# A hybrid decoder step: sixteen prompt-only FFN tiles, the sample rows' chain pinned step by step between the prompt's matmuls, and the prompt's query blocks attended in the order 3, 2, 1, 0

## The chip, the cores and the metric

The kernel runs on one core of one Trainium2 chip. The metric is the device time in microseconds (us) of one execution, taken as the median of three runs. Beside these runs stands one profiled execution, from which every duration below is read. The engines are called PE (TensorE; PEld is its weight load), DVE (VectorE), ACT (ScalarE), POOL (GpSimd) and SP (SyncE, which only issues DMAs).

## The reference, cut to what matters

One layer of a decoder is computed for two groups of tokens with the same weights: a prompt of 512 tokens, and a sample group of 8 sequences with 4 new tokens each (32 rows), which have 4096 cached positions behind them in a paged cache.

```python
def hybrid_layer(x, pos0, attend, lru_buf, lru_h0, ffn_buf, lw):
    ...
    h = rmsnorm(x, norm_mix_g)
    q, k, v, qi, ki, wi, xl, gl, ga, gb = split_cols(h @ w_in, IN_SPLITS)
    ...
    y_a = attend(q, k, v, qi, ki, wi).reshape(B, T, ATTN_WIDTH) @ w_proj_a
    xc, lru_buf_new = causal_dwconv(xl, lru_buf, lru_conv_w, lru_conv_b)
    hl, h_last = rg_lru(xc, lru_h0, lru_wa, lru_ba, lru_wx, lru_bx, lru_lambda)
    y_b = (hl * jax.nn.gelu(gl)) @ w_proj_b
    x = x + (jax.nn.sigmoid(ga) * y_a + jax.nn.sigmoid(gb) * y_b) @ w_out
    h = rmsnorm(x, norm_ffn_g)
    ua, ub = split_cols(h @ w_up, (D_FF, D_FF))
    uc, ffn_buf_new = causal_dwconv(ua, ffn_buf, ffn_conv_w, ffn_conv_b)
    x = x + (jax.nn.gelu(uc) * ub) @ w_down
```

`attend` is sparse in both groups. A small indexer scores every position, and each query attends only to its best ones: of the 512 prompt positions the best 128, of the 4100 sample positions the best 256. For a sample row the 256 selected keys and values lie anywhere in `cache_k` and `cache_v`, so they have to be gathered row by row (512 numbers each, 8 heads of 64). D is 1024, the FFN is 3072 wide, and the outputs also hold keys, values and states.

## The kernel before, in words

Everything is one program for a tile framework, which schedules the instructions of each engine by a simulated timeline: `tc.high_priority(n)` raises the priority of what stands inside, and `tc.issue_after(x)` puts an instruction behind x. Each engine then takes its instructions in that fixed order; each tile pool has a number of buffers, and a load waits until its buffer is free.

Large matmuls are three passes over operands split into a high and a low part: a chunk of weights is loaded on SP's queue into `wr` (3 buffers), ACT casts it to `wh` (L167), DVE subtracts to get `wl` (L168; two buffers each), and PE multiplies high by high, high by low and low by high.

In the order of time:

1. *Projections, recurrence, index scores, prompt attention.* Prompt attention is done in units of a query block i (128 rows; block i sees i + 1 blocks of keys) and some heads: four heads in a unit for i = 0 and 1, two for i = 2 and 3. A unit multiplies queries and keys (L542), adds the mask (L933), makes probabilities (L935 to L942), transposes them (L948) and multiplies them with the values (L963). The units of i = 0, 1 and 2 run as a pipeline among other projections; then comes the projection of the recurrent branch with its gates, and the four units of i = 3 at a higher priority. Beside this, DVE selects each sample row's 256 positions.
2. *proj_a and w_out.* The attended rows are split into `yahi` and `yalo`, multiplied with w_proj_a in eight tiles (L1005 to L1007), gated, and multiplied with w_out (L233 to L235). Meanwhile the selected positions are turned into row numbers `idx`: PE spreads them by one-hot matmuls (L867), and DVE (L871) and ACT (L873) reduce 64 blocks of them.
3. *Norm and prompt-only FFN tiles.* Of the 24 tiles of 128 FFN columns the first NP = 12 are computed for the prompt's 512 rows alone: `form_p` (L258 to L260) makes 24 matmuls of 512 columns for each of the two halves of w_up, DVE convolves (L1243, L1245) and gates (L1259), and after each four tiles `form_a` multiplies with their rows of w_down (2 x 48 matmuls of 512 columns, L233 to L235) and DVE adds the result to the rows (L1265).
4. *The sample rows' chain*, beside stage 3 at a low priority (PRIO // 10): for each of the 32 sample rows (a "key" below is one such row with its 256 gathered cached keys) POOL issues two gathers of 128 cached rows (L1067), which wait until the norms' last power on POOL (`normed`) is past. The scores of a key are made in one of three ways, by a table of letters: P (10 keys), PE transposes the rows (L1100), ACT copies them (L1101), PE multiplies (L1109); A (6 keys), DVE multiplies with the broadcast query (L1118) and ACT sums over 64 elements (16 instructions, L1122); D (16 keys), DVE multiplies (L1118) and DVE reduces (L1125). Then follow a softmax for each half of the rows (L1131 to L1150), eight steps of values with eight gathers each (L1174), folds (L1162, L1185), w_proj_a and w_out for these rows and their norm. Only then are the sample rows ready for the FFN.
5. *Shared tiles.* The other 12 tiles are computed for prompt and sample rows together: `form_b` (L248 to L250) makes 24 matmuls of 256 columns and 24 of 288 for each half of w_up. What the sample rows still lack of the first 12 tiles is made by `rows_by_columns` (L278; bursts of 32 small matmuls over 512 KB of weights, loaded on SP's queue at L271 into `sw`, three buffers), one step of `sample_steps` behind each shared tile. At the end come the first half of w_down for the 12 tiles, its last half (L1421, L1428 to L1430) and the final norm.

Of the kernel before, what the change touches and what calls it, by code (L numbers as in the profile page):

```python
# [18 lines left out]
D = 1024  # L19
SEQ = 512  # L20
# [8 lines left out]
NP = 12  # L29
# [67 lines left out]
def build(tc, I, O, dbg=None, mark=lambda n: None):  # L97
# [16 lines left out]
    with outer:  # L114
# [32 lines left out]
        WAYS = "PDDPPDDPDDDPADAPDDDPDAAPDDAPDDDP"  # L147
# [67 lines left out]
        def form_a(w, nk, a_hi, a_lo, a_s, col0, ncol, kc):  # L215
# [5 lines left out]
            for k0 in range(0, nk, kc):  # L221
# [7 lines left out]
                for t in range(4):  # L229
                    sl = slice(t * 128, (t + 1) * 128)  # L230
                    for k in range(kc):
# [3 lines left out]
                        T.matmul(out[t], a_lo[:, kk, sl], hi[:, k, :], start=False, stop=kk == nk - 1)  # L235
# [17 lines left out]
        def form_p(w, col0, a_hi, a_lo, ps, first=None):  # L253

            b = ps()
            _, hi, lo = first or columns(w, 8, col0)
            for k in range(8):
                T.matmul(b, hi[:, k, :], a_hi[:, k, :SEQ], start=k == 0, stop=False)  # L258
                T.matmul(b, hi[:, k, :], a_lo[:, k, :SEQ], start=False, stop=False)  # L259
                T.matmul(b, lo[:, k, :], a_hi[:, k, :SEQ], start=False, stop=k == 7)  # L260
            return b

        def rows_by_columns(a_s, nk, mk, w, col0, burst):
# [3 lines left out]
            for k0 in range(0, nk, burst):  # L267
                rows = []
                for k in range(k0, k0 + burst, 2):
                    raw = mk((128, 2, 512))  # L270
                    nc.sync.dma_start(raw, w[k * 128:(k + 2) * 128, col0:col0 + 512].rearrange("(k p) c -> p k c", p=128))  # L271
                    rows += [raw[:, 0], raw[:, 1]]
                order = list(range(k0, k0 + burst))[::-1]
                head = None
                for k in order:
                    for c in range(4):
                        with tc.issue_after(head.ins) if head else ExitStack():
                            m = T.matmul(b[32 * c:32 * c + 32, :128], a_s[:, k, :], rows[k - k0][:, c * 128:(c + 1) * 128],  # L278
                                         start=k0 == 0 and k == order[0], stop=k0 + burst == nk and k == order[-1],
                                         tile_position=(0, 32 * c))  # L280
                        head = head or m
# [121 lines left out]
        kih = mp.tile([128, SEQ], F32R, name="kih")  # L403
# [434 lines left out]
        with tc.high_priority(PRIO // 10):  # L838
# [15 lines left out]
            scr2 = CW((128, 512), F16)  # L854
            for h4 in range(2):
# [5 lines left out]
                for t in range(4):  # L861
# [3 lines left out]
                    for j in range(2):  # L865
                        for bi in range(4):
                            T.matmul(bs[j][:, bi * 128:(bi + 1) * 128], oh[32 * t:32 * t + 32, bi, j * 128:(j + 1) * 128],  # L867
                                     M[32 * t:32 * t + 32, h4 * 4 + bi, 0:128], start=True, stop=True, tile_position=(32 * t, 0))
# [9 lines left out]
                    V.scalar_tensor_tensor(ix, phys, float(PG), slot, op0=ALU.mult, op1=ALU.add)  # L878

            vms = CW((128, 2, 288), BF16)  # L880
# [589 lines left out]
```

## Time and profile before

| | us |
|---|---|
| three runs | 1070.83, 1074.62, 1075.09 |
| median | 1074.62 |
| profiled execution | 1077.11 |
| its span (first to last instruction) | 1075.0 |
| PE busy in the span | 1007.3 |
| DVE busy | 695.9 |
| ACT busy | 425.4 |
| POOL busy | 187.9 |

The mean granted clock of TensorE was 0.968 of full speed. In the profile's rows the engine, line, operation, tiles and shapes come first. In the groups, behind the bar, stand the busy time in us, the mean of one in ns, and the engine's idle time just before them with what ended most of it. In the timeline the columns are the start, the duration, the instruction and its count, with the idle time before it in square brackets. PE's matmuls overlap, so their durations add up to more than the time between their starts.

### The profile page before, as it was taken

The page shows a single profiled execution, that of the slowest core. Times are in us where ns is not written, and L with a number is a line of the kernel's source. Part 1 is how long each engine was busy: PE and PEld are TensorE (multiplying, and loading weights), DVE is VectorE, ACT ScalarE, POOL GpSimd, SP SyncE. Part 2 cuts the span into 40 slices and gives each one's busy share as a digit, 9 for nine tenths or more (in the row PEclk, how much of TensorE's full clock was granted, in tenths as well). Part 3 has the DMA queues.
Part 4 walks back from the last instruction along what each step waited for, and adds up shares of the span by engine and source line. Part 5 has one row for each costly group of instructions (what it writes and reads, how often), then busy time and mean ns, then how long its engine had stood idle before and what let it go on. Part 6 is the DMA issues. An engine that isn't in the chain of part 4 may idle for free.

```text
span 1075.0 us, 19144 instructions
## 1 busy us (share of the span) xinstructions
PE 1007.3 (94%) x7516; PEld 825.3 (77%) x7516; DVE 695.9 (65%) x1517; ACT 425.4 (40%) x973; POOL 187.9 (17%) x183
## 2 busy tenths in 40 slices
PE   5999999999999997899789799869999999999997
PEld 4877988987788985677657576456688999999785
DVE  6655998999998857676668764333555454546352
ACT  5232654632365456343336643121332332324331
POOL 3420000001200000000568764635000000000000
PEclk9998999999999999799899899889999999999999
DMA  7751313336342334473488885755773776561401
GB/s 261 219 163 36 91 52 97 101 101 208 116 128 81 97 105 132 113 273 102 132 260 263 288 251 170 234 145 171 241 245 108 232 223 218 156 222 62 143 22 62
DMA packets 143141, 170.03 MB, mean 158 GB/s; under 512 B 12348, under 2 KB 94396, under 8 KB 143052
## 3 DMA queue, kind: packets, MB, share of 16 engines
q1 hardware_dynamic: 118952, 109.24, 33.1%
q0 software_dynamic: 12864, 42.75, 12.6%
q10 hardware_dynamic: 11236, 16.82, 5.0%
q8 instruction: 59, 0.97, 0.4%
q14 instruction: 30, 0.25, 0.1%
HBM read 159.10 MB, written 9.68 MB: 157 GB/s over the span
## 4 chain that ended last, share of the span: by engine, by line
PE 45%; DMA 5%; issue 4%; DVE 3%; POOL 1%; ACT 1%; another core or an unknown queue 1%; ACTq 0%; POOLq 0%; DVEq 0%; SPq 0%
DMA cg<-in_cache_k_dram,idx 2%; PE pd L233 2%; PE pd L235 2%; PE pd L234 2%; PE pc L278 2%; PE pa L248 2%; PE pa L250 2%; PE pd L248 2%; PE pa L249 2%; PE pd L249 2%; PE pd L250 2%; PE pa L258 1%; PE pd L258 1%; PE pa L259 1%; PE pa L260 1%
## 5 line engine op out<-in xcount | busy, mean ns | idle before, releaser
L167 ACT CAST wh<-wr 128x1024 fp32r<-128x1024 f32 (+1 forms) x124 | 123.0, 993 | 284.6 <-PE pd L235 67.8
L168 DVE TENSOR_TENSOR wl<-wr,wh 128x1024 fp32r<-128x1024 f32 (+1 forms) x124 | 143.1, 1154 | 132.9 <-ACT wh L167 119.8
L248 PE MATMUL pd<-hhi,wh 128*128 128x256 f32 (+1 forms) x384 | 114.4, 298 | 0.0
L250 PE MATMUL pd<-hhi,wl 128*128 128x256 f32 (+1 forms) x384 | 114.0, 297 | 0.0
L249 PE MATMUL pd<-hlo,wh 128*128 128x256 f32 (+1 forms) x384 | 112.5, 293 | 0.0
L176 POOL TENSOR_TENSOR smn<-smn,mhalf 128x1 f32<-128x1 f32 (+1 forms) x15 | 10.3, 687 | 460.8 <-DVE smn L1410 262.5
L1067 POOL DMA_INDIRECT cg<-in_cache_k_dram,idx x64 | 78.3, 1224 | 28.1 <-issue 15.8
L250 PEld LDWEIGHTS pd<-hhi,wl 128*128 128x128 f32 x384 | 72.8, 190 | 4.8 <-issue 3.2
L248 PEld LDWEIGHTS pd<-hhi,wh 128*128 128x128 f32 x384 | 72.8, 190 | 3.2 <-issue 1.9
L249 PEld LDWEIGHTS pd<-hlo,wh 128*128 128x128 f32 x384 | 72.9, 190 | 2.9 <-issue 2.5
L1067 POOL DMA_INDIRECT cg<-in_cache_v_dram,idx x48 | 50.0, 1041 | 28.5 <-issue 14.7
L377 POOL TENSOR_TENSOR pw<-pw,pw 128x512 f32<-128x512 f32 x8 | 11.2, 1397 | 198.4 <-DVE pw L374 197.0
L248 PE MATMUL pa<-mhi,wh 128*128 128x288 f32 (+1 forms) x144 | 42.2, 293 | 0.0
L250 PE MATMUL pa<-mhi,wl 128*128 128x288 f32 (+1 forms) x144 | 42.1, 293 | 0.0
L249 PE MATMUL pa<-mlo,wh 128*128 128x288 f32 (+1 forms) x144 | 42.1, 293 | 0.0
L248 PE MATMUL pd<-mhi,wh 128*128 128x256 f32 (+1 forms) x144 | 41.6, 290 | 0.0
L249 PE MATMUL pd<-mlo,wh 128*128 128x256 f32 (+1 forms) x144 | 41.4, 288 | 0.0
L250 PE MATMUL pd<-mhi,wl 128*128 128x256 f32 (+1 forms) x144 | 41.1, 288 | 0.0
L258 PE MATMUL pa<-mhi,wh 128*128 128x512 f32 x96 | 39.7, 413 | 0.0
L260 PE MATMUL pa<-mhi,wl 128*128 128x512 f32 x96 | 39.0, 406 | 0.4 <-issue 0.4
L259 PE MATMUL pd<-mlo,wh 128*128 128x512 f32 x96 | 38.9, 405 | 0.5 <-issue 0.5
L779 DVE MAX8 cw<-cg 128x8 f32<-128x1028 f32 x32 | 39.2, 1225 | 0.2
(604 smaller groups left out, 2831.1 us busy)
## 6 DMA issues: line engine op xcount, KB each, us to landing
wr<-in_w_up_dram SPq DMA_DIRECT2D x48, 512.0 KB
wr<-in_w_in_dram SPq DMA_DIRECT2D x36, 512.0 KB
sw<-in_w_up_dram SPq DMA_DIRECT2D x24, 512.0 KB
wr<-in_w_down_dram SPq DMA_DIRECT2D x18, 512.0 KB
cg<-in_w_in_dram SPq DMA_DIRECT2D x12, 512.0 KB
sw<-in_w_down_dram SPq DMA_DIRECT2D x12, 512.0 KB
xb<-qsd ACTq DMA_DIRECT2D x22, 256.0 KB
wr<-in_w_out_dram SPq DMA_DIRECT2D x8, 512.0 KB
```

The lines of the kernel that those rows point to most:

```text
L167: S.copy(hi, raw)
L168: V.tensor_tensor(lo, raw, hi, op=ALU.subtract)
L233: T.matmul(out[t], a_hi[:, kk, sl], hi[:, k, :], start=kk == 0, stop=False)
L234: T.matmul(out[t], a_hi[:, kk, sl], lo[:, k, :], start=False, stop=False)
L248: T.matmul(b, hi[:, k, :], a_hi[:, k, c0:c1], start=k == 0, stop=False)
L249: T.matmul(b, hi[:, k, :], a_lo[:, k, c0:c1], start=False, stop=False)
L250: T.matmul(b, lo[:, k, :], a_hi[:, k, c0:c1], start=False, stop=k == nk - 1)
L258: T.matmul(b, hi[:, k, :], a_hi[:, k, :SEQ], start=k == 0, stop=False)
L259: T.matmul(b, hi[:, k, :], a_lo[:, k, :SEQ], start=False, stop=False)
L260: T.matmul(b, lo[:, k, :], a_hi[:, k, :SEQ], start=False, stop=k == 7)
L779: V.max(top[:, 8 * r:8 * r + 8], src)
L1067: G.indirect_dma_start(out=kt[0][j], out_offset=None, in_=src, in_offset=IndirectOffsetOnAxis(ap=idx[q // 16, q % 4][:, j, q // 4 % 4:q // ...
```

## The change

It has five parts.

1. NP goes from 12 to 16: sixteen prompt-only tiles (four groups of four), eight shared tiles. `sample_steps` now has eleven steps for eight shared tiles (before nine for twelve); those left over run behind the last tile. `rows_by_columns` for the first tiles' w_up and w_down grows from 18 to 24 bursts.
2. The way P is gone. All 32 keys are multiplied on DVE (L1122 after); every third is summed on ACT (10 keys, L1127), the other 22 are reduced on DVE (L1131).
3. The chain becomes a generator, `sample_chain`. The prompt's loop takes a step of it after each half of a tile and two after each half of w_down (12 steps in a group of four tiles), and `behind` puts each step's first instructions on PE, DVE and ACT behind the newest of the prompt's there. Gathers are asked for up to six places ahead (a key takes one place, a value step three) and no longer wait for the norm; the values of the first half come between the keys of the second. The w_proj_a and w_out rows of the chain are loaded on POOL's queue instead of SP's.
4. Choosing the indices becomes a generator, `choose`, with one step behind each of proj_a's last four tiles and each quarter of w_out's first half, and the rest behind w_out.
5. The prompt's units are attended in the order i = 3, 2, 1 in the pipeline, and i = 0 (two units of four heads) at the end at the higher priority. `form_p` makes the first tile in two halves of 256 columns.

```diff
-NP = 12
+NP = 16
...
-        WAYS = "PDDPPDDPDDDPADAPDDDPDAAPDDAPDDDP"
...
-            pipeline([(i, h0, (4, 4, 2)[i]) for i in range(3) for h0 in range(0, 8, (4, 4, 2)[i])], PA)
+            pipeline([(i, h0, (4, 4, 2, 2)[i]) for i in (3, 2, 1) for h0 in range(0, 8, (4, 4, 2, 2)[i])], PA)
...
-            pipeline([(3, h0, 2) for h0 in range(0, 8, 2)], PA)
+            pipeline([(0, h0, 4) for h0 in range(0, 8, 4)], PA)
...
+                if ft >= 4:
+                    with tc.high_priority(PRIO // 10 - 3 * PRIO):
+                        next(chosen, None)
...
+        def key_scores(q, kt, qb, act):
+            g, q16 = q // 16, q % 16
+            with behind("V"):
+                V.tensor_tensor(kt, kt, qb[:, None, :].to_broadcast([128, 2, 512]), op=ALU.mult)
+            if act:
+                for j in range(2):
+                    for h in range(8):
+                        with behind("A"):
+                            S.activation(junk, kt[:, j, h * 64:(h + 1) * 64], AF.Copy,
+                                         accum_out=sT[:, g, j, q16, h:h + 1])
+            else:
+                with behind("V"):
+                    V.tensor_reduce(sT[:, g, :, q16, :], kt.rearrange("p j (h d) -> p j h d", h=8), axis=AX.X,
+                                    op=ALU.add)
...
+            order = (0, 4, 8, 12, 1, 5, 9, 13, 2, 6, 10, 14, 3, 7, 11, 15)
+            turns = [("K", q) for q in order]
+            for g8 in range(4):
+                turns += [("K", 16 + q) for q in order[4 * g8:4 * g8 + 4]] + [("V", g8)]
+            turns += [("V", g8) for g8 in range(4, 8)]
+            asked, room = [], 6
...
+            for fl in range(n):
                 ft = f0 + fl
...
+                pa = form_p(w_up, ft * 128, h2hi, h2lo, PD, None if ft else first[0], ft == 0)
+                turn["T"] = newest[0]
...
+                turn["V"] = V.tensor_copy(fsp[:, ft], xb[:, 512:514])
                 gated_up(ft, fl, Gh, Gl, xb, uc)
-                S.activation(uc, uc, AF.Gelu_apprx_tanh)
+                next(chain, None)
+                ub = form_p(w_up, DFF + ft * 128, h2hi, h2lo, PA, None if ft else first[1], ft == 0)
+                turn["T"] = newest[0]
+                turn["A"] = S.activation(uc, uc, AF.Gelu_apprx_tanh)
                 V.tensor_tensor(uc, uc, ub, op=ALU.mult)
-                split_act(Gh[:, fl], Gl[:, fl], uc)
+                S.copy(Gh[:, fl], uc)
+                turn["V"] = V.tensor_tensor(Gl[:, fl], uc, Gh[:, fl], op=ALU.subtract)
+                next(chain, None)
```

What this does to the order of the instructions is shown at three places. First PE at the end of the prompt attention. Before, behind the last matmuls with the gates' weights (L248 to L250), there are only sample projections (L278) and the transposes and value products (L948, L963) of the last units of i = 3:

```order
L248 MATMUL pd_5218<-hbhi,wh_5221 128x288
L249 MATMUL pd_5218<-hblo,wh_5221 128x288
L250 MATMUL pd_5218<-hbhi,wl_5222 128x288
L278 MATMUL pc_3180<-cg_3185,hs_137 32x128
L948 MATMUL pa_5369<-cst,pw_5294 128x128 x4
L278 MATMUL pc_3180<-cg_3185,hs_137 32x128 x4
L948 MATMUL pa_5376<-cst,pw_5304 128x128 x4
```

Of the change, the same engine from the last unit's transposes to the first matmul of proj_a (L965, L980 and L1022 are the transposes, value products and proj_a there):

```order
L965 MATMUL pa_5224<-cst,pw_5190 128x128
L980 MATMUL pa_5229<-pw_5225,vv 64x128
L980 MATMUL pa_5229<-pw_5220,vv 64x128
L980 MATMUL pa_5229<-pw_5225,vv 64x128
L816 MATMUL pc_3233<-cst,cw_3226 128x32 x4
L281 MATMUL pc_3239<-cg_3246,hs_137 32x128 x8
L281 MATMUL pc_3239<-cg_3244,hs_137 32x128 x8
L281 MATMUL pc_3239<-cg_3242,hs_137 32x128
L832 MATMUL pc_3293<-smc_3287,cst 128x1
L281 MATMUL pc_3239<-cg_3242,hs_137 32x128
L1022 MATMUL pd_5251<-yahi,wh_5254 128x512
```

The last unit has one block of keys where it had four, and sample projections stand between it and proj_a. Second DVE in the second prompt-only tile. Before (L168 splits weights, L1118 and L1125 are a key's multiplication and reduction, `pw` is the tile):

```order
L168 TENSOR_TENSOR wl_7128<-wr_7125,wh_7127 128x1024
L1118 TENSOR_TENSOR cg_6226<-cg_6226,xb_6229 128x1024
L1259 TENSOR_TENSOR pw_7082<-pw_7082,pa_7056 128x512
L1118 TENSOR_TENSOR cg_6233<-cg_6233,xb_6236 128x1024
L1125 TENSOR_REDUCE sTP<-cg_6226 128x2x8
L155 TENSOR_TENSOR Gp_7030<-pw_7082,Gp_7029 128x512
L168 TENSOR_TENSOR wl_7171<-wr_7168,wh_7170 128x1024
L1118 TENSOR_TENSOR cg_6255<-cg_6255,xb_6258 128x1024
```

And of the change (L167 splits weights, L1122 and L1131 are a key's two steps, L1337 and L1339 are a tile's gating and split):

```order
L1122 TENSOR_TENSOR cg_5991<-cg_5991,xb_6189 128x1024
L167 TENSOR_TENSOR wl_6431<-wr_6428,wh_6430 128x1024
L1337 TENSOR_TENSOR pw_6288<-pw_6288,pa_6317 128x512
L1131 TENSOR_REDUCE sT<-cg_5991 128x2x8
L1339 TENSOR_TENSOR Gp_6129<-pw_6288,Gp_6128 128x512
L1122 TENSOR_TENSOR cg_5997<-cg_5997,xb_6295 128x1024
L1122 TENSOR_TENSOR cg_6000<-cg_6000,xb_6352 128x1024
L167 TENSOR_TENSOR wl_6473<-wr_6470,wh_6472 128x1024
```

Keys stand between the tile's steps in both; of the change, there are 15 of them up to the end of the fourth tile's w_down, and the other 17 behind it. Third SP's queue near the end. Before, the sample rows' chunks of w_down (`sw`) are asked for between prompt chunks of w_up (`wr`):

```order
L271 DMA sw_9740<-in_w_down_dram 128x2x512
L271 DMA sw_9896<-in_w_down_dram 128x2x512
L164 DMA wr_10228<-in_w_up_dram 128x8x128
L271 DMA sw_9898<-in_w_down_dram 128x2x512
L271 DMA sw_9916<-in_w_down_dram 128x2x512
```

Of the change they stand behind the last chunk of w_up, among the prompt's chunks of w_down (`ft`, and the last `wr`):

```order
L1477 DMA ft_1731_10587<-in_w_down_dram 128x512
L1477 DMA ft_1732_10588<-in_w_down_dram 128x512
L274 DMA sw_10253<-in_w_down_dram 128x2x512
L274 DMA sw_10276<-in_w_down_dram 128x2x512
L274 DMA sw_10278<-in_w_down_dram 128x2x512
L274 DMA sw_10296<-in_w_down_dram 128x2x512
L274 DMA sw_10298<-in_w_down_dram 128x2x512
L274 DMA sw_10316<-in_w_down_dram 128x2x512
L163 DMA wr_10533<-in_w_down_dram 128x2x512
L274 DMA sw_10318<-in_w_down_dram 128x2x512
```

All sixteen have moved from beside the tiles of w_up to beside the last matmuls with w_down.

More of the change, by code (lines that the diff above doesn't have):

```diff
@@ L854, in build, with behind, choose @@
             scr2 = CW((128, 512), F16)
+        turn = {}
+        def behind(eng):
+            return tc.issue_after(turn[eng].ins) if eng in turn else ExitStack()
+        def choose():
             for h4 in range(2):
@@ L991, in build @@
             yalo = mp.tile([128, 4, SEQ], F32R, tag="y2", name="yalo")
-            for i in range(4):
+            for i in (3, 2, 1, 0):
                 tq = slice(i * 128, (i + 1) * 128)
@@ L1033, in build @@
                             T.matmul(out[t], mhi[:, kk, sl], los[kk], start=False, stop=False)
-                            T.matmul(out[t], mlo[:, kk, sl], his[kk], start=False, stop=kk == 7)
+                            turn["T"] = T.matmul(out[t], mlo[:, kk, sl], his[kk], start=False, stop=kk == 7)
+                    if c == 0:
+                        with tc.high_priority(PRIO // 10 - PRIO // 3):
+                            next(chosen, None)
                 if c == 0:
@@ new lines, in softmax, with fold @@
+            T.transpose(b[:32, 256:384], p[:, 256:288], ident)
+            S.copy(pT[:, g], b[:, :256].rearrange("p (j c) -> p j c", j=2))
+            S.copy(pTn[:, g, :], b[:32, 256:384])
+            yield
+        def fold(b, selm, first):
+            ym = CW()
+            V.tensor_tensor(ym, b, C("mh"), op=ALU.mult)
+            yield
+            b2 = PC()[:, :128]
+            head = None
+            for c in range(4):
+                with tc.issue_after(head.ins) if head else behind("T"):
+                    m = T.matmul(b2[32 * c:32 * c + 32], selm, ym[:, c * 128:(c + 1) * 128], start=True, stop=True,
+                                 tile_position=(0, 32 * c))
+                head = head or m
+            if first:
+                V.tensor_copy(yrows, b2)
+            else:
+                V.tensor_tensor(yrows, yrows, b2, op=ALU.add)
@@ new lines, in values, with column @@
+        def values(g8, vts):
+            b = PC()
+            def column(c, j):
+                return T.matmul(b[32 * c:32 * c + 32, :], pT[:, g8 // 4, j, (g8 % 4) * 32:(g8 % 4 + 1) * 32], vts[c][j],
+                                start=j == 1, stop=j == 0, tile_position=(0, 32 * c))
+            with behind("T"):
+                head = column(3, 1)
+            with tc.issue_after(head.ins):
+                for c, j in ((0, 1), (1, 1), (2, 1), (3, 0), (0, 0), (1, 0), (2, 0)):
+                    column(c, j)
+            yield from fold(b, C("sel", g8 * 32, g8 * 32 + 32), False)
```

352 lines of the change are left out of this document (183 added, 169 removed).

## The prediction

> **What bounds the kernel now.** I read the page first: its totals, then its slices.
>
> ```profile
> span 1075.0 us, 19144 instructions
> PE 1007.3 (94%) x7516; PEld 825.3 (77%) x7516; DVE 695.9 (65%) x1517; ACT 425.4 (40%) x973; POOL 187.9 (17%) x183
> PE   5999999999999997899789799869999999999997
> ```
>
> TensorE (PE) is busy for 94% of the span, so time can be won only by giving it less to do or by filling its holes. The slices show the holes in the sixteenth to thirtieth fortieths, that is between some 400 and 800 us. I cut the span at the stages (the windows; the columns are us, then busy time and count of PE, PEld, DVE, ACT and POOL, then the granted clock, the DMA share and GB/s).
>
> ```profile
> 0.00:408.10 408.10, 391.74 (x3253) 332.76 (x3253) 332.20 (x763) 190.60 (x403) 38.70 (x45) 0.99 0.41 123
> 408.10:430.40 22.30, 15.64 (x201) 11.38 (x201) 17.32 (x37) 14.93 (x39) 0.00 (x0) 0.88 0.49 149
> 430.40:502.60 72.20, 69.41 (x305) 51.32 (x306) 51.03 (x166) 29.46 (x95) 0.00 (x0) 0.92 0.57 181
> 502.60:631.00 128.40, 108.75 (x508) 82.75 (x507) 96.05 (x142) 63.39 (x214) 83.39 (x71) 0.91 0.71 222
> 631.00:822.40 191.40, 177.65 (x1038) 126.07 (x1036) 82.13 (x143) 50.95 (x75) 63.10 (x62) 0.96 0.63 196
> 822.40:1031.00 208.60, 207.79 (x1980) 191.49 (x1978) 101.83 (x229) 66.09 (x129) 0.00 (x0) 1.00 0.53 168
> 1031.00:1075.00 44.00, 36.37 (x241) 29.49 (x240) 15.37 (x43) 9.99 (x23) 2.74 (x5) 0.94 0.15 51
> ```
>
> The seven stages are: everything up to the last gate projection; the tail of the prompt attention; proj_a and w_out; the norm and the first four prompt-only tiles with all key scores; the other eight with the values; the twelve shared tiles with the first half of their w_down; the last half and the final norm. The clock is below 0.97 exactly in the four middle stages, with 6.7, 2.8, 19.7 and 13.8 us of idle PE. A hole costs twice, because matmuls behind it run slowly:
>
> ```profile
> 430.40 1.22 PE L1005 MATMUL pd<-yahi,wh 128*128 128x512 f32 x2 [2.63 <-ACT yahi L154]
> 431.42 0.63 PE L1006 MATMUL pd<-yalo,wh 128*128 128x512 f32 x1
> 431.85 0.63 PE L1007 MATMUL pd<-yahi,wl 128*128 128x512 f32 x1
> 651.02 0.39 PE L258 MATMUL pd<-mhi,wh 128*128 128x512 f32 x1
> 651.25 0.39 PE L259 MATMUL pd<-mlo,wh 128*128 128x512 f32 x1
> 853.65 0.30 PE L248 MATMUL pd<-mhi,wh 128*128 128x288 f32 x1
> 853.79 0.30 PE L249 MATMUL pd<-mlo,wh 128*128 128x288 f32 x1
> 856.01 0.28 PE L248 MATMUL pd<-mhi,wh 128*128 128x256 f32 x1
> 856.13 0.28 PE L249 MATMUL pd<-mlo,wh 128*128 128x256 f32 x1
> ```
>
> From start to start a 512-column matmul takes 0.43 us after the idle and 0.23 us at full clock; ends overlap, so I count starts. Over a run of 24 I get 0.2335, and for the two halves of a shared tile 0.1175 (256 columns) and 0.1335 (288).
>
> **The change part by part.** The sum is made against the profiled execution (1077.11 us, span 1075.0), which stands 2.49 us above the median of 1074.62; its seven windows are the seven terms. The first, 408.1 us, I leave alone: the attention units there only swap places, and the mask of the last block of rows, which the first unit now needs, is there in time:
>
> ```profile
> L764 DVE TENSOR_SCALAR mask<-acc_all x3: 282/357/417, 164.7 to 244.1; 128x256 bf16<-128x256 f32 x1, 128x384 bf16<-128x384 f32 x1, 128x512 bf16<-128x512 f32 x1
> L933 DVE CUSTOM_DVE_ANT_0 pw<-pa,cst x8: 268/284/292, 291.8 to 306.9; 128x128 f32<-128x128 f32 x8
> ```
>
> The last mask is made at 244.1, and the first unit of before adds its mask at 291.8.
>
> *Attention tail, proj_a, w_out (94.5 us): -9.* In the tail PE waits again and again for a DVE or ACT step of two-head units four blocks wide. The units that now come last are one block wide, and their products run beside gate matmuls; I take 22.3 us down to 18. Choosing the indices leaves the first four tiles of proj_a. In this window half of its 64 passes are on DVE, the others on ACT:
>
> ```profile
> L871 DVE TENSOR_SCALAR_CACHE_REDUCE cw<-pc,cst 128x127 f16<-128x127 f32 x32 | 9.4, 347 | 2.9 <-PE pc L867 2.8
> ```
>
> More than half of them move behind w_out, to where DVE is needed (below). The proj_a tiles wait less for their own DVE steps: of the 2.8 us of idle PE and the 6 that a clock of 0.92 costs in 72.2, I take 5 as won. Range -15 to +3: the upper end is for choosing delaying the norm.
>
> *Norm and first four tiles (128.4 us): -18.* Ten keys lose their transposes and products on PE, and every key is now multiplied on DVE:
>
> ```profile
> L1100 PE MATMUL pc<-cst,cg 128*128 128x128 f32 x80 | 13.1, 297 | 6.0 <-ACT ft L1101 5.1 <-DMA cg<-in_cache_k_dram,idx 0.9
> L1109 PE MATMUL pc<-ft,cw 128*32 128x256 f32 x80 | 10.8, 383 | 0.5 <-ACT pw L1258 0.5
> L168 DVE TENSOR_TENSOR wl<-wr,wh 128x1024 fp32r<-128x1024 f32 x36 | 44.0, 1222 | 42.2 <-ACT wh L167 29.4 <-issue 6.4 <-PE pc L1100 4.5
> L1118 DVE TENSOR_TENSOR cg<-cg,xb 128x1024 f32<-128x1024 f32 x22 | 26.8, 1220 | 18.4 <-DMA cg<-in_cache_k_dram,idx 17.9 <-issue 0.2
> L1125 DVE TENSOR_REDUCE sTP<-cg 128x16 f32<-128x1024 f32 x17 | 20.6, 1212 | 0.1
> L1245 DVE SCALAR_TENSOR_TENSOR pw<-pw,fv,pw 128x512 f32<-128x512 f32 x24 | 18.0, 748 | 0.5
> L1259 DVE TENSOR_TENSOR pw<-pw,pa 128x512 f32<-128x512 f32 x12 | 8.2, 684 | 27.4 <-remote 11.7 <-PE pa L260 9.1 <-ACT pw L1258 6.5
> ```
>
> Removed from PE: 24 us of overlapping records, about 17 from start to start, and 6.5 of waits. What stays on PE by the new order is 4 x 48 x 0.2335 + 96 x 0.2335 = 67.2 plus the norm's transposes and late w_out and index matmuls, about 85 us. DVE, in its new order from the first eviction of w_out's last half to the end of this group, has 15 multiplications and 14 weight splits at 1.22 (35.4), 10 reductions at 1.21 (12.1), per tile two steps at 0.75 and three at 0.68 (14.2 for four), 20 evictions and splits 512 wide at 0.68 (13.6), four norm products taken at 1.22 (4.9), about 25 index passes at 0.35 (8.7) and, an estimate, 13 of small steps: 102 us. So DVE, not PE, ends this stage; I add 8 us for waits and slow matmuls and take 110. The other 17 keys move to the second group, where DVE, counted in the same way, has about 52 us of work beside 74 of PE. Bounds: 102 without a wait, and 123 if the gather wait of 17.9 above returns with most of its length (-26 to -5). Queued behind a multiplication that waits for its gather stand weight splits and tile steps, and PE behind those; gathers are now asked six slots ahead and no longer after the norm, hence less of it.
>
> *The other prompt-only tiles: +49.* They were eight in 191.4 us and are twelve. Tiles: 12 x 48 x 0.2335 = 134.5, three groups' w_down 3 x 96 x 0.2335 = 67.2. The chain puts onto PE eight value steps:
>
> ```profile
> 670.31 0.43 PE L1162 MATMUL pc<-cw,cst 128*32 128x128 f32 x8
> 670.56 0.59 PE L1174 MATMUL pc<-ft,cw 128*32 128x512 f32 x1
> 672.39 0.50 PE L259 MATMUL pa<-mlo,wh 128*128 128x512 f32 x1
> PE pc L1133 <- issue: 8.6, 6, 1.9
> PE pc L1174 <- DMA cg<-in_cache_v_dram,idx: 4.4, 1, 4.4
> ```
>
> From 670.56 to 672.39 is 1.83 each: 14.7. Folds, softmaxes, new keys, projection and the rows' w_out I take as 15, of the 20 that the window of before has beyond its tiles, values, idle time and slow clock (191.4 - 134.5 - 14.7 - 13.8 - 8). That makes 231.5. Waits: this window's 13.8 of idle held 8.6 for which the profile names no releaser and 4.4 for a value gather; since matmuls are now pinned one tile apart I take 8 in all, so 240. Range 234 to 252 (+43 to +61): no wait, or these waits and again as much.
>
> *The shared tiles and the first half of w_down (208.6 us): -47.* Twelve become eight: 8 x 2 x 24 x (0.1175 + 0.1335) = 96.4. The first half of w_down falls from 144 matmuls to 96, 22.4. The sample rows' bursts rise from 18 to 24, of which 22 lie here (15 before):
>
> ```profile
> 851.21 1.08 PE L278 MATMUL pc<-sw,h2s 128*32 128x128 f32 x32
> 951.22 8.25 SPq L271 DMA_DIRECT2D sw<-in_w_down_dram  x4
> 1031.03 1.95 PE L1421 MATMUL pc<-ft,Gs 128*32 128x128 f32 x64
> ```
>
> A burst of 32 takes about 1.04, so they are 22.9. Before has 14.8 beyond tiles, w_down and bursts (208.6 - 144.6 - 33.6 - 15.6), and I keep two thirds of it, 10, for eight tiles of twelve: 152. New is a wait: eleven sample steps now hang on eight tiles, so w_down's sample loads are asked for after the last w_up tile, sixteen through three slots, in front of the last prompt chunk in SP's queue. The row of 951.22 says 8.25 us for four such loads; sixteen are 33 us and some 3 MB of prompt weights come on top, beside 39 us of PE work. I take 10 us of wait, range 2 to 20. So 162: -47, range -55 to -37.
>
> *The end (44.0 us): -12.* Before has three bursts (3.1), 144 matmuls (33.6) and 7.3 for the final norm. After: two bursts (2.1), 96 matmuls (22.4) and 7.3 again: 31.8.
>
> Sum: -9 - 18 + 49 - 47 - 12 = -37, so 1040 for the profiled execution and 1038 against the median. More prompt-only tiles are no gain in themselves: four tiles save 4 x 2 x 24 x (0.251 - 0.2335) = 3.4 of PE, and six more bursts cost 6.2. The gain is 17 of PE work gone, and holes closed.
>
> **A rule weighed.** The two-input multiplication on DVE runs beside gathers that POOL issues:
>
> ```profile
> L1118 DVE TENSOR_TENSOR cg<-cg,xb x22: 1211/1221/1227, 531.2 to 624.8; 128x1024 f32<-128x1024 f32 x22
> L1067 POOL DMA_INDIRECT cg<-in_cache_k_dram,idx x64: 942/947/2708, 520.7 to 626.0; - x64
> L1067 POOL DMA_INDIRECT cg<-in_cache_k_dram,idx x64 | 78.3, 1224 | 28.1 <-issue 15.8
> ```
>
> The Trainium skill, "SBUF — State Buffer", section "Who interferes with whom", says that a DVE instruction with two SBUF inputs contends with a GpSimd instruction that reads SBUF, and that the second to start blocks fully; by it the sum would get up to 15 x 0.95 = 14 us on DVE in the first group. The trace does not agree on DVE's side, where the longest of 22 multiplications is 1227 ns, 6 above the median. POOL does pay: the mean gather is 277 ns over the median, 18 us over 64. All 128 issues at 1.22 + 0.3 are 195 us, which the 320 us of the two stages cover, so I add nothing.
>
> **The rivals.**
>
> *All holes close.* DVE hides, no gather is late, the tail's loads keep up: the lower bounds of the five terms give -15 - 26 + 43 - 55 - 12 = -65, 1012 us, 1010 against the median. Against it: engines take their work in order, and no middle stage of before ran without a hole. Chance 0.08.
>
> *The holes only move.* The gathers' waits return on DVE, the value steps wait, and the tail waits 20: +3 - 5 + 61 - 37 - 12 = +10 if all happen; half of it is some -13, 1061 us against the median. For it speaks that DVE carries 102 of the first 110 us. Chance 0.10 for 1056 to 1080.
>
> *Slower: VectorE paces the first two groups.* In-order queueing there means that each of 32 multiplications may hold splits for the next tile's weights. If each key costs PE 1.2 us beyond the first group's 102, that is 38 us, with half of it again as matmuls at 0.43 instead of 0.23: some 50 us against the sum, 1088 us. It decides from about 42 us on. For it: the second wait of L1259's row (9.1 for PE) shows engines that already wait for each other in turn, and the stage's clock was 0.91. Against it: two split weight tiles stand ahead of PE, and the second group has 52 us of DVE beside 74 of PE. Chance 0.10.
>
> *The change doesn't do what it says:* the order shows that it does; no chance given.
>
> **How the numbers follow.** Forecast 0.72, centred on 1038, its own range 1018 to 1058. A run tells about 0.5% from no change, 5.4 us: faster is below 1069, slower above 1080. Faster: 0.72 + 0.08 + 0.04 of the second rival = 0.84; same: 0.06 of that rival; slower 0.10. The range 1012 to 1068 leaves out the slower rival, the upper part of the second and the end of the first.
>
> **What would show it.** Right: no transposes of gathered keys on PE; a first group of 105 to 120 us with DVE above 90% busy; prompt-only tiles ending near 800 to 815 us; a wait of some 10 us for the sample loads of w_down before the last 60 us. Wrong: a clock below 0.9 over the second group, DVE waits for gathered keys above 20 us in sum, or a value gather that PE waits for more than twice.

## The result and the profile after

The changed kernel takes 1039.05 us in the median of four runs (1036.57 to 1044.51), beside 1072.72 for the kernel before in the same runs: a ratio of 0.9696, 95% interval 0.9641 to 0.9751. The forecast was 1038. The profiled execution took 1044.51 us, which is the longest of the four, and this matters below.

The page of the changed kernel, its totals and the slices of PE:

```profile
span 1042.7 us, 18950 instructions
PE 981.3 (94%) x7342; PEld 803.1 (77%) x7342; DVE 711.2 (68%) x1506; ACT 441.1 (42%) x1101; POOL 204.7 (20%) x197
PE   5999999999999998999899999999989999999586
```

The holes between 400 and 800 us are nearly gone, and a new one, deeper than those, stands in the last fortieths. PE is busy 26 us less, and the span is 32 us shorter. The same seven stages (the third ends 9.4 us ahead of the norm's first transposes, as it did before):

```profile
0.00:407.60 407.60, 391.61 (x3301) 334.25 (x3301) 333.84 (x769) 195.68 (x409) 40.79 (x45) 1.00 0.40 122
407.60:420.60 13.00, 10.37 (x121) 6.93 (x120) 9.07 (x22) 7.84 (x26) 0.00 (x0) 0.74 0.83 290
420.60:482.80 62.20, 60.55 (x289) 46.34 (x289) 46.04 (x92) 23.11 (x48) 13.57 (x12) 1.00 0.72 243
482.80:583.00 100.20, 93.06 (x474) 76.99 (x473) 82.52 (x193) 57.98 (x216) 37.38 (x32) 0.95 0.54 170
583.00:833.60 250.60, 241.57 (x1268) 175.34 (x1269) 150.10 (x222) 98.81 (x288) 110.22 (x105) 0.97 0.70 224
833.60:1008.80 175.20, 158.54 (x1708) 142.59 (x1708) 74.95 (x168) 49.13 (x98) 0.00 (x0) 0.94 0.62 198
1008.80:1042.70 33.90, 25.66 (x193) 20.62 (x192) 14.64 (x43) 8.57 (x19) 2.76 (x5) 0.94 0.22 81
```

| stage | before | after | difference | forecast |
|---|---|---|---|---|
| up to the last gate matmul | 408.1 | 407.6 | -0.5 | 0 |
| attention tail, proj_a, w_out | 94.5 | 75.2 | -19.3 | -9 |
| norm and first four tiles | 128.4 | 100.2 | -28.2 | -18 |
| the other prompt-only tiles | 191.4 | 250.6 | +59.2 | +49 |
| shared tiles, first half of w_down | 208.6 | 175.2 | -33.4 | -47 |
| the end | 44.0 | 33.9 | -10.1 | -12 |
| span | 1075.0 | 1042.7 | -32.3 | -37 |

So the sum came out, but by misses of 10 to 14 us that cancel: the first stages won more, the last ones less. That the total lies within 1 us of the forecast is luck. In PE's waits from 407 us on, the three longest rows are:

```profile
PE pc L281 <- DMA sw<-in_w_down_dram: 13.7, 7, 4.7
PE pc L1178 <- DMA cg<-in_cache_v_dram,idx: 5.0, 2, 3.5
PE pc L226 <- DMA wr<-in_w_down_dram: 2.8, 1, 2.8
```

The first and the third are the wait that the prediction had added, for w_down's sample loads and the prompt chunk queued behind them on SP. The timeline of PE shows them:

```profile
979.02 1.08 PE L281 MATMUL pc<-sw,Gs 128*32 128x128 f32 x32 [3.75 <-DMA sw<-in_w_down_dram]
984.78 1.93 PE L281 MATMUL pc<-sw,Gs 128*32 128x128 f32 x32 [4.68 <-DMA sw<-in_w_down_dram]
989.72 1.94 PE L281 MATMUL pc<-sw,Gs 128*32 128x128 f32 x32 [3.00 <-DMA sw<-in_w_down_dram]
998.61 1.08 PE L226 MATMUL pc<-wr,Gs 128*32 128x128 f32 x16 [2.85 <-DMA wr<-in_w_down_dram]
```

```profile
979.00:980.10 1.10, 1.08 (x32) 0.81 (x32) 0.00 (x0) 0.00 (x0) 0.00 (x0) 1.00 0.95 331
984.70:986.70 2.00, 1.92 (x32) 1.38 (x32) 0.00 (x0) 0.00 (x0) 0.00 (x0) 0.50 0.11 35
```

The first burst still takes 1.08 us, at a granted clock of 1.00; the next two take 1.93 and 1.94, the one in the second window at 0.50. So all but the first of these holes are paid a second time.

### The profile page after: what moved, and what is told of

Same layout as the page of the kernel before. It is cut to its first block, busy times and chain, and to the rows that moved or that the text cites. A ratio compares the mean times of both kernels' runs of the same rounds, so it can differ in the third digit from the quotient of the medians.

```text
span 1042.7 us, 18950 instructions
## 1 busy us (share of the span) xinstructions
PE 981.3 (94%) x7342; PEld 803.1 (77%) x7342; DVE 711.2 (68%) x1506; ACT 441.1 (42%) x1101; POOL 204.7 (20%) x197
## 3 DMA queue, kind: packets, MB, share of 16 engines
q1 hardware_dynamic: 119432, 109.24, 33.9%
## 4 chain that ended last, share of the span: by engine, by line
PE 78%; DMA 8%; DVE 6%; issue 3%; ACT 2%; POOL 2%; another core or an unknown queue 1%; SPq 0%; POOLq 0%; DVEq 0%; ACTq 0%
PE pd L248 7%; PE pd L247 7%; PE pd L249 7%; PE pc L281 3%; PE pd L232 3%; PE pd L233 3%; PE pd L234 3%; PE pd L260 3%; PE pa L262 3%; PE pa L260 3%; PE pa L261 3%; PE pd L261 2%; PE pd L262 2%; PE pa L545 2%; DMA sw<-in_w_down_dram 2%
## 5 line engine op out<-in xcount | busy, mean ns | idle before, releaser
L167 DVE TENSOR_TENSOR wl<-wr,wh 128x1024 fp32r<-128x1024 f32 (+1 forms) x126 | 145.3, 1153 | 102.3 <-ACT wh L166 90.9
L248 PE MATMUL pd<-hlo,wh 128*128 128x256 f32 (+1 forms) x384 | 112.2, 292 | 0.0
L1095 POOL DMA_INDIRECT cg<-in_cache_k_dram,idx x64 | 75.6, 1181 | 156.6 <-issue 101.6
L248 PEld LDWEIGHTS pd<-hlo,wh 128*128 128x128 f32 x384 | 72.3, 188 | 2.8 <-issue 2.7
L1095 POOL DMA_INDIRECT cg<-in_cache_v_dram,idx x48 | 55.3, 1151 | 20.3 <-issue 12.2
L260 PE MATMUL pd<-mhi,wh 128*128 128x512 f32 (+1 forms) x136 | 53.4, 392 | 1.2 <-DVE xa L1346 1.2
L262 PE MATMUL pa<-mhi,wl 128*128 128x512 f32 (+1 forms) x136 | 53.1, 390 | 1.3 <-DVE wl L167 1.3
L261 PE MATMUL pd<-mlo,wh 128*128 128x512 f32 (+1 forms) x136 | 53.0, 390 | 0.2 <-issue 0.2
L260 PE MATMUL pa<-mhi,wh 128*128 128x512 f32 (+1 forms) x136 | 52.9, 389 | 0.0
L262 PE MATMUL pd<-mhi,wl 128*128 128x512 f32 (+1 forms) x136 | 52.5, 386 | 0.2 <-issue 0.2
L261 PE MATMUL pa<-mlo,wh 128*128 128x512 f32 (+1 forms) x136 | 52.5, 386 | 0.0
L1127 ACT ACTIVATE junk<-cg 128x64 f16<-128x64 f32 x160 | 40.9, 256 | 23.8 <-DVE cg L1122 10.1
L1122 DVE TENSOR_TENSOR cg<-cg,xb 128x1024 f32<-128x1024 f32 x32 | 38.6, 1223 | 2.4 <-DMA xb<-qsd 2.4
L233 PE MATMUL pd<-wl,Gp 128*128 128x512 f32 x96 | 37.7, 393 | 0.0
```

Source lines behind the costliest of these rows:

```text
L167: V.tensor_tensor(lo, raw, hi, op=ALU.subtract)
L233: T.matmul(out[t], a_hi[:, kk, sl], lo[:, k, :], start=False, stop=False)
L248: T.matmul(b, hi[:, k, :], a_lo[:, k, c0:c1], start=False, stop=False)
L260: T.matmul(b[:, c0:c1], hi[:, k, :], a_hi[:, k, c0:c1], start=k == 0, stop=False)
L261: T.matmul(b[:, c0:c1], hi[:, k, :], a_lo[:, k, c0:c1], start=False, stop=False)
L262: newest[0] = T.matmul(b[:, c0:c1], lo[:, k, :], a_hi[:, k, c0:c1], start=False, stop=k == 7)
```

## The experiments

Three chips were used. On the first the kernel before took 1071.86 us, on the second 1055.80 and on the third 1055.58, so results are compared by their ratio to before on the same chip. (The chip of the result above is not on record; before took 1072.72 there, as on the first.) The ratios are given as recorded, and can differ from the quotient of the medians by up to 0.4%. The changed kernel was run again, as the yardstick, on the second chip. On the first chip ran the old order, the order alone, the twelve tiles and the first try with two sample steps; on the third the chain unpinned alone, the early choosing, the late gathers and the six buffers; the others on the second.

**The changed kernel again.**

> The changed kernel once more, unchanged, for a second profile beside the variants. Its profiled execution took 1044.5 where its other runs took 1036.6 to 1041.5, and held one stretch of 10 us between 757 and 768 us in which TensorE waited for values. Theory (that stretch comes and goes with the execution): 1036 to 1040, and a profile without it. Rival (it belongs to the kernel): the stretch stands at the same place.

Measured: 1029.58 us, ratio 0.9732 (0.9684 to 0.9780). In the first profile TensorE took 10 us over value matmuls that need 1.83:

```profile
757.85 0.59 PE L1178 MATMUL pc<-cg,cw 128*32 128x512 f32 x1 [0.17 <-issue]
760.30 0.59 PE L1178 MATMUL pc<-ft,cw 128*32 128x512 f32 x1 [1.43 <-issue]
763.09 2.46 PE L1178 MATMUL pc<-cg,cw 128*32 128x512 f32 x3 [1.50 <-DMA cg<-in_cache_v_dram,idx]
765.89 1.01 PE L1178 MATMUL pc<-cg,cw 128*32 128x512 f32 x1 [0.34 <-issue]
```

In the second profile the windows of the first group, of the other prompt-only tiles and of the shared tiles read:

```profile
484.90:586.80 101.90, 93.30 (x474) 76.93 (x473) 82.28 (x193) 57.96 (x216) 35.76 (x32) 0.95 0.54 172
586.80:823.70 236.90, 234.59 (x1273) 175.63 (x1274) 150.27 (x224) 99.32 (x289) 108.04 (x105) 0.99 0.73 235
823.70:994.90 171.20, 155.49 (x1697) 140.04 (x1696) 74.74 (x166) 48.94 (x98) 0.00 (x0) 0.96 0.63 202
```

The stretch is not there, and without it the other prompt-only tiles take 236.9 us, 3 less than forecast. The theory said that it comes and goes with the execution, and two profiles can't tell that from another cause, since the chip changed too. The other profiles point to the chip. On the first chip three of the four, also that of the kernel before with the new order alone, hold a seventh value step of 7.6 to 8.1 us, and all four hold idle time of TensorE between 580 and 815 us, beside the prompt-only tiles, for which no releaser is named, 1.5 to 8.8 us in sum. Its longest rows with two sample steps, and with the new order alone:

```profile
PE pc L1178 <- issue: 2.0, 3, 0.8
PE pc L1174 <- issue: 2.5, 3, 1.5
```

The eight profiles of the other two chips have none. Whether one and the same chip can show both was not tried. The waits of the tail are there in both profiles of the changed kernel.

**The old order of query blocks, all else as changed; and the new order alone in the kernel before.**

```diff
-            pipeline([(i, h0, (4, 4, 2, 2)[i]) for i in (3, 2, 1) for h0 in range(0, 8, (4, 4, 2, 2)[i])], PA)
+            pipeline([(i, h0, (4, 4, 2)[i]) for i in range(3) for h0 in range(0, 8, (4, 4, 2)[i])], PA)
...
-            pipeline([(0, h0, 4) for h0 in range(0, 8, 4)], PA)
+            pipeline([(3, h0, 2) for h0 in range(0, 8, 2)], PA)
```

> The changed kernel with the prompt's query blocks in the old order again (0, 1, 2 in the pipeline, 3 at the end), all else as changed. Theory (three sources: order, choosing moved, keys off TensorE): the stretch from the last gate matmul to the first proj_a matmul goes back from 13.0 to about 22 us, nothing else moves, so 1048 us, 9 above the changed kernel's 1039. Rival (the tail of the attention is hidden in what follows, and the gain there comes from choosing alone): 1039 to 1042.

> The kernel before with the order 3, 2, 1, 0 alone. Theory: the same 9 us off, 1064 beside a before of 1073. Rival (with choosing still between proj_a's tiles, DVE and ACT are late there whatever ends the attention): 1070 to 1073.

Measured: 1041.78, ratio 0.9741 (0.9676 to 0.9805), with the old order back; 1077.33, ratio 1.0014 (0.9967 to 1.0060), with the new order alone. The first windows of the kernel with the old order back, tail and then proj_a with w_out (to the last w_out matmul), and below them the same two of the new order alone:

```profile
404.30:421.60 17.30, 14.33 (x194) 10.63 (x193) 13.47 (x27) 11.82 (x30) 0.00 (x0) 0.90 0.62 191
421.60:504.70 83.10, 76.39 (x325) 57.42 (x326) 53.83 (x135) 28.22 (x67) 17.85 (x18) 0.96 0.62 214
```

```profile
413.90:431.50 17.60, 13.68 (x181) 9.62 (x179) 15.05 (x42) 12.49 (x44) 0.00 (x0) 0.85 0.60 192
431.50:516.30 84.80, 80.09 (x366) 60.45 (x367) 61.06 (x192) 35.72 (x106) 1.11 (x2) 0.95 0.51 160
```

In the changed kernel the two are 13.2 and 74.4 us, in the kernel before 22.3 and 84.3:

```profile
420.60:495.00 74.40, 72.75 (x346) 56.36 (x346) 51.53 (x105) 28.20 (x56) 18.62 (x18) 1.00 0.69 233
430.40:514.70 84.30, 81.51 (x361) 61.25 (x362) 59.33 (x188) 34.49 (x103) 1.11 (x2) 0.93 0.49 155
```

In the tail each part has its own price: 22.3 us as before, 17.6 with the new order alone, 17.3 with the rest of the change alone (the old order back), 13.2 with both. Proj_a and w_out get short with both together only: 84.3, 84.8, 83.1 and 74.4. But ahead of the tail the new order costs something. In the changed kernel the last gate matmul comes at 407.4 us instead of 404.3; with the order alone it comes at 413.9, where two profiles with the old order have 407.9 and 403.6. So the old order reaches the FFN 10 us later, and yet the whole time differs by 2.7 us only, within the intervals. The theory of 9 us falls, and the order alone is worth nothing that can be measured. Later stages give most of the 10 us back. Which of them, these runs don't show: from the first FFN matmul to the first shared tile it takes 323.5 us with the old order, and 319 to 334 in four profiles with the new one and the same code there.

**Twelve prompt-only tiles.**

```diff
-NP = 16
+NP = 12
```

> The changed kernel with twelve prompt-only tiles again: 36 turns instead of 48 for the chain, what is left of it runs bare behind the last of them, and nine sample steps hang on twelve shared tiles. Theory (the tiles are hosts for the chain): the tail's 16 us wait for w_down's sample loads goes, but the last 10 or so steps of the chain, four value steps among them, run with nothing between, some 25 us with a lowered clock: 1045 to 1055. Rival (more prompt-only tiles are no gain in themselves, the gain is in keys and pinning): 1025 to 1035, since the tail is mended.

Measured: 1052.64, ratio 0.9830 (0.9762 to 0.9899), 13.6 above the changed kernel. Four rows of PE's waits show what ran bare behind the last prompt-only tile, all but 3 us of the first row:

```profile
PE pc L1178 <- DMA cg<-in_cache_v_dram,idx: 8.7, 3, 5.8
PE pc L1166 <- DVE cw L1160: 8.5, 3, 6.4
PE pc L281 <- DMA cg<-in_w_out_dram: 8.5, 4, 3.3
PE pc L208 <- DVE cg L192: 5.2, 1, 5.2
```

They are 30.9 us, 28 of them behind that tile, and of the waits for w_down's sample loads 0.8 us is left. So sixteen tiles are worth about 14 us net, as places for the chain's 48 turns, not as tiles.

**Two sample steps behind each of the first three shared tiles.**

```diff
-                next(steps, None)
+                for _ in range(2 if fl < 3 else 1):
+                    next(steps, None)
```

> The changed kernel with two sample steps behind each of the first three shared tiles, so that all eleven steps have a tile. Theory (the tail waits because w_down's sample loads are asked for behind the last w_up tile): the waits for sample loads of w_down, 13.7 us, and the slow matmuls behind them go, 1024 to 1030. Rival (the stage is bound by the bytes it loads, so that the wait moves to the loads of w_up for the first three tiles): 1036 to 1042.

Measured: 1031.99, ratio 0.9644 (0.9588 to 0.9700), 7 us under the changed kernel, less than expected, and the intervals of the two ratios overlap. The waits for w_down's sample loads are gone, and half as much has come up in their place:

```profile
PE pc L281 <- DMA sw<-in_w_up_dram: 7.2, 6, 2.1
```

The theory holds for the cause of the wait, the rival for half of its size.

**All reductions on VectorE.**

```diff
-                    key_scores(n, rows, qb, done % 3 == 0)
+                    key_scores(n, rows, qb, False)
```

> The changed kernel with all 32 reductions on VectorE and none on ScalarE: five more reductions at 1.21 us in the first group of four tiles, five behind it. Theory (VectorE ends the first group): that group takes 5 to 6 us more, the second absorbs its share, 1043 to 1046 beside the changed kernel's 1039. Rival (TensorE ends it, since its matmuls ran without holes over most of the group): the same within 2 us.

Measured: 1031.50, ratio 0.9750 (0.9712 to 0.9789) beside 0.9732. The windows of this kernel's first group and of its other prompt-only tiles:

```profile
484.70:585.70 101.00, 90.81 (x474) 74.64 (x473) 86.75 (x197) 39.49 (x96) 41.48 (x33) 0.98 0.53 170
585.70:822.60 236.90, 235.06 (x1273) 175.40 (x1274) 156.85 (x230) 65.67 (x88) 114.68 (x104) 0.99 0.72 236
```

VectorE has 4.5 us more to do in the first group and 6.6 behind it (82.28 to 86.75, 150.27 to 156.85), and both stages take as long as without (101.9 and 236.9). The theory falls: VectorE's work does not set how long the first group takes.

**Nothing pinned; then the chain alone unpinned.**

```diff
         def behind(eng):
 
-            return tc.issue_after(turn[eng].ins) if eng in turn else ExitStack()
+            return ExitStack()
```

> The changed kernel with nothing pinned behind the prompt's newest instruction, for the chain and for choosing alike: the scheduler places them by priority alone. Theory (the pinning closes holes, because a step in the queue that waits for its gather holds everything behind it): more waits of TensorE for value gathers and for splits, 15 to 25 us slower than the changed kernel, 1055 to 1063. Rival (gathers that are asked for early suffice, and the scheduler orders as well): 1036 to 1044.

Measured: 1073.64, ratio 1.0151 (1.0099 to 1.0203): some 44 us above the changed kernel and slower than the kernel before. More than expected, and in another place: from the last w_out matmul to the first one of the FFN it takes about 35 us, in the changed kernel 5. In the second kernel choosing stays pinned (`tc.issue_after(turn["T"].ins)` in place of its two `behind("T")`):

> The changed kernel with the chain's steps unpinned and choosing still pinned. Without both pins the norm took 31 us more (from the last matmul of w_out to the first of the FFN 35.7 where it was 5.0) and the first group 18 more. Theory (two separate holes, one for each pin): the norm is as in the changed kernel, the first group again near 100 us, so a ratio to before of 0.985 to 0.99. Rival (choosing alone is what the pin keeps out of the way, and the late first group only follows from it): 0.970 to 0.975.

Measured: 1071.90, ratio 1.0145 (1.0092 to 1.0199). Neither theory nor rival: the chain's pins carry the whole difference, the norm's part too. The windows of this kernel from the last w_out matmul to the first of the FFN, and of the first group behind it:

```profile
498.00:534.10 36.10, 11.86 (x69) 9.18 (x67) 33.56 (x98) 28.07 (x149) 28.26 (x24) 0.54 0.75 241
534.10:634.00 99.90, 85.58 (x417) 65.34 (x416) 64.74 (x103) 46.64 (x164) 41.15 (x37) 0.91 0.57 173
```

PE has 11.86 us of work in 36.1, and VectorE is busy for 33.56. The timeline of VectorE just ahead of it says with what:

```profile
490.20 0.68 DVE L1067 TENSOR_TENSOR xa<-pa,xa 128x512 f32<-128x512 f32 x1
490.80 1.20 DVE L1131 TENSOR_REDUCE sT<-cg 128x16 f32<-128x1024 f32 x1
491.93 0.67 DVE L1067 TENSOR_TENSOR xa<-pd,xa 128x512 f32<-128x512 f32 x1
492.73 0.15 DVE L183 TENSOR_SCALAR smn<-smn 128x1 f32<-128x1 f32 x1
492.92 0.15 DVE L176 TENSOR_SCALAR smn<-smn 128x1 f32<-128x1 f32 x1
496.83 1.22 DVE L1122 TENSOR_TENSOR cg<-cg,xb 128x1024 f32<-128x1024 f32 x1 [3.76 <-DMA cg<-in_cache_k_dram,idx]
497.98 0.68 DVE L1067 TENSOR_TENSOR xb__5573<-pd,xb__5573 128x512 f32<-128x512 f32 x1
```

Keys stand in VectorE's queue between the evictions of w_out (L1067) and the norm's small steps; at 496.83 one waits 3.76 us for its gather, and the next eviction of the norm's input waits behind it. Over the whole run such multiplications wait 21.1 us for gathered keys:

```profile
L1122 DVE TENSOR_TENSOR cg<-cg,xb 128x1024 f32<-128x1024 f32 x32 | 39.1, 1222 | 23.7 <-DMA cg<-in_cache_k_dram,idx 21.1 <-DMA xb<-qsd 2.4
```

In the changed kernel they never do (its row stands further down), and the first key is multiplied at 523.8 us, behind the first tile's pin.

**The way P taken out of the kernel before.**

```diff
-        WAYS = "PDDPPDDPDDDPADAPDDDPDAAPDDAPDDDP"
+        WAYS = "DDA" * 10 + "DD"
```

> The kernel before with a table of ways without P: 22 keys reduced on VectorE and 10 summed on ScalarE, as in the change, and nothing else. Theory (TensorE loses 17 us of work, but in the old order all 32 keys fall into the first group, where VectorE then has about 115 us): the gain is eaten by VectorE, 1065 to 1078 beside 1072. Rival (TensorE's work alone counts): 1052 to 1058.

Measured: 1050.67 beside 1055.80 for before, ratio 0.9969 (0.9932 to 1.0005). Right as to size: 17 us less for TensorE are worth 5 us by the medians, at most 7 by the interval. That VectorE eats the rest was not shown: no profile of before was taken on this chip.

**Choosing in all of proj_a; gathers asked for three places ahead.**

```diff
-                if ft >= 4:
-                    with tc.high_priority(PRIO // 10 - 3 * PRIO):
-                        next(chosen, None)
+                with tc.high_priority(PRIO // 10 - 3 * PRIO):
+                    next(chosen, None)
```

> The changed kernel with one step of choosing behind each of all eight proj_a tiles, pinned as changed, so that the indices are ready before w_out. Theory (choosing beside proj_a's gating delays its tiles, as in before): 6 to 9 us more from the first proj_a matmul to the last of w_out (76 in the changed kernel), of which the norm and the first group, freed of choosing, give back 5: 0 to 5 us slower, ratio 0.97 to 0.978. Rival (the pin alone keeps choosing harmless wherever it stands, and earlier gathers help): 5 us faster, 0.965.

```diff
-            asked, room = [], 6
+            asked, room = [], 3
```

> The changed kernel with gathers asked for three places ahead instead of six, so that of value steps only one is asked for at a time. Theory (asking early is what ends the waits for gathers): TensorE waits for each of the eight value steps' gathers, 8 x 1.25 us of issue and some 2 to 3 us of landing less what lies beside one tile, about 3 us a step with slow matmuls behind: 20 to 30 us slower, ratio 0.99 to 1.0. Rival (a step in the queue every half tile hides a gather that is asked for one step ahead): within 5 us, 0.97 to 0.976.

Measured: 1028.32, ratio 0.9724 (0.9672 to 0.9775), and 1027.67, ratio 0.9730 (0.9679 to 0.9781): both the same as the changed kernel's 0.9732. Where choosing stands within proj_a and w_out makes no difference, and neither does asking early. The first ratio lies within its theory's range, but the 6 to 9 us that the theory looked for are not there: from the first proj_a matmul to the last of w_out it takes 75.7 us, and 76.7 in the changed kernel's second profile. For the gathers the theory falls clearly. This kernel's waits for value gathers:

```profile
PE pc L1178 <- DMA cg<-in_cache_v_dram,idx: 2.4, 2, 1.9
```

**Two steps behind the second, fourth and sixth shared tile, and six buffers.**

```diff
-        SW = maker(pool(ffn, "sw", 3), "sw")
+        SW = maker(pool(ffn, "sw", 6), "sw")
...
-                next(steps, None)
+                for _ in range(2 if fl in (1, 3, 5) else 1):
+                    next(steps, None)
```

> The changed kernel with two sample steps behind the second, fourth and sixth shared tile and six buffers for their loads instead of three. Two steps behind the first three tiles with three buffers ended the waits for w_down and left 7.2 us of waits for w_up. Theory (those came from three buffers, through which SP asks too late): they go as well, ratio to before 0.955 to 0.960. Rival (the stage's bytes bound it): as with two steps and three buffers, 0.964.

Measured: 1013.60, ratio 0.9583 (0.9541 to 0.9625), where the changed kernel has 0.9732 on this chip: 16 us less, and faster than both kernels. Its window of the shared tiles with the first half of w_down, and the wait that is left there:

```profile
821.00:978.70 157.70, 152.47 (x1740) 139.79 (x1738) 77.08 (x172) 48.91 (x97) 0.00 (x0) 1.00 0.64 212
PE pc L281 <- DMA sw<-in_w_up_dram: 4.3, 2, 2.3
```

The window falls from 171.2 to 157.7 us, and its clock rises from 0.96 to 1.00. The bytes do not bound this stage; three buffers and the order of asking did. How much each of the two is worth was not tried: the places of the steps changed along with the buffers.

## Why the prediction was right, point by point

*Attention tail, proj_a, w_out (-9, measured -19).* The mechanism is half shown, and the term was mis-sized. The order's part of the tail came out as costed: with the order alone the tail takes 17.6 us, where the forecast was 18. But everything ahead of the tail was left alone as a mere swap of places, and there the order costs 3 us or more by these profiles; alone it gives a ratio of 1.0014. The 5 us for the place of choosing have no price of their own: choosing can stand in all of proj_a at 0.9724. Of the 19 us, 9 came in the tail, half by the order and half by the rest of the change, and 10 in proj_a and w_out, where only both together win anything. Of what the order adds to that, 10 us, little is left in the time.

*Norm and first group (-18, measured -28).* Here a step failed: "So DVE, not PE, ends this stage". With 4.5 us more on VectorE in the group, it takes no longer. The count of 102 us was too high besides: VectorE is busy for 82.5 of the stage's 100.2 us. It runs with hardly a gap from 521 to 575 us (51.2 of 54), but 13 of the 15 keys counted are multiplied before the stage ends, and neighbouring steps overlap a little. The keys at the end of its queue are due only for the softmax of the next group, and here such a backlog delayed nobody. PE had 85 us by the same paragraph; 93 of 100.2 are busy. That the gathers' waits would go was right, though not for the reason given: asking three places ahead does as well as six. With six places no multiplication waits for a gather, with three they wait 2 us in sum, and without the pins 21.1. What ended the waits is the pins, which keep every key behind the first tile.

*The other prompt-only tiles (+49, measured +59 and, on the second chip, 236.9 us where the forecast was 240).* Right; the profiled execution held the 10 us stretch. The profile of before had held one too, and the prediction took most of its 8.6 us as gone. The sentence that these tiles would end near 800 to 815 us was a slip against the text's own terms, which give 844; it was 833.6 and 823.7.

*Shared tiles (-47, measured -33).* The new wait was foreseen with its cause and place, and mis-sized. PE waits 16.5 us for the loads, not 10, and slow bursts and matmuls behind the waits bring it to about 23 (175.2 beside the 152 of work), past the range of 2 to 20; in the second profile it is 19. Spreading the steps removes the waits for w_down, which shows the cause. Of the bursts of small matmuls, three were taken from the wrong line: those of the last 44 us (L1421) belong to the last half of w_down. All 18 bursts of before's sample steps lie in the shared stage, and 23 of the changed kernel's 24. With these counts the stage's work comes to some 150.5 us instead of 152.

*The end (-12, measured -10).* Right.

*The signs.* Two of the four signs of being right came: no gathered key is transposed on PE, and PE waits for the sample loads of w_down. The first group was to take 105 to 120 us with VectorE above 90% busy, and took 100.2 at 82%; the fourth is the slip on 800 to 815 us. None of the signs of being wrong came. One reading was off: the clock is below 0.97 in the last stage of before too (0.94), not only in the four middle ones.

*More tiles "are no gain in themselves".* Right, but it hid what they are for. With twelve tiles the same chain is 13.6 us slower, though the tail's wait is gone, because its last turns have no host.

*The rule weighed.* The groups of the changed kernel, multiplications on VectorE and gathers of keys on POOL:

```profile
L1122 DVE TENSOR_TENSOR cg<-cg,xb 128x1024 f32<-128x1024 f32 x32 | 38.6, 1223 | 2.4 <-DMA xb<-qsd 2.4
L1095 POOL DMA_INDIRECT cg<-in_cache_k_dram,idx x64 | 75.6, 1181 | 156.6 <-issue 101.6
```

With 32 multiplications instead of 22 beside the gathers the mean is 1223 ns after 1220, and the longest 1274. VectorE is not held up here either, so adding nothing for the rule of the Trainium skill, "SBUF — State Buffer", section "Who interferes with whom", was right on VectorE's side. A gather takes 1181 ns in the mean; that the multiplications lengthen it was not tried by itself.

*Where the gain came from.* Shown: without the chain's pins the change loses 42 to 44 us and is slower than before; without the four tiles it loses 14; taking P out of before is worth at most 7; the order, the place of choosing, asking early and the way of reducing are worth nothing measurable by themselves. The pin of choosing was never taken out alone; without the chain's pins it makes no difference (ratios 1.0151 and 1.0145). The kernel before had its own guard for the norm (gathers waited for the norm's last power); the change drops it, and the pins have to do its work and then space the keys over two groups. How the 26 to 28 us on the second chip divide between P, the spacing and the tiles beyond these figures stays open.

## What to carry to other kernels

Before an engine is named as the bound of a stage, ask who waits for the work at the end of its queue: a backlog that is due only in the next stage can be free, however full the engine looks. Low-priority work on engines that run in order needs a place, not only a priority: one gather that is late holds up everything queued behind it, and here pinning each step behind the main work's newest instruction was worth 42 to 44 us, asking for the data early nothing. When work loses hosts, count the steps against the hosts that are left, and give a stage of loads enough buffers that SP can ask ahead.

## What the runs showed of the hardware that was not expected

In two profiles, of before (703.7 to 713.5 us) and of the changed kernel (757.9 to 767.8 us), TensorE takes about 10 us for a few small matmuls, with gaps of up to 1.9 us before single instructions, while POOL issues value gathers one after another. For most of these gaps the profile names no releaser. Between 580 and 815 us such gaps come to 9.3 and 2.3 us in these two profiles, to 1.5 to 8.8 in the four of the first chip, and to nothing in the eight of the other two. What they are remains open.

The first chip is 1.5% slower than the other two on the kernel before (1071.86 us beside 1055.80 and 1055.58), which is half of what this change is worth. The stretch may be part of that, which these runs don't show.
